# Thresholded attention on one core: the last two groups' queries taken by one-hot products instead of indirect gathers, with a new order of steps

## The chip, the cores and the metric

The kernel runs on one core of one Trainium2 chip. The metric is device time in microseconds (us), lower is better. The engines are named as in the profile: PE (TensorE: matmuls, with PEld for its weight loads), DVE (VectorE), ACT (ScalarE), POOL (GpSimd), SP (SyncE, which here only issues DMA transfers). Each engine takes its instructions in the order in which they were written; the engines wait for each other by semaphores.

## What is computed

```python
batch, heads, seq, dim = 8, 12, 512, 64          # Q, K, V: float32, random normal
scores = np.einsum('bhqd,bhkd->bhqk', Q, K) * (1.0 / np.sqrt(dim))
weights = softmax(scores)                        # exp, max taken off, divided by the row's sum
weights = np.where(weights > threshold, weights, 0)          # threshold = 0.1
weights = weights / (weights.sum(axis=-1, keepdims=True) + 1e-10)
return np.einsum('bhqk,bhkd->bhqd', weights, V)
```

There are 96 heads of 512 queries and 512 keys. A weight of over 0.1 among 512 is rare. Most rows of the output are zero, and a row that is not zero is nearly always one row of V.

## The kernel before, in words

The kernel uses this. It first finds the few query rows ("hits") that can have a weight over the threshold, with cheap arithmetic over all scores; then it does those rows again in float32, finds the key, and copies that row of V to the output. Everything else in the output is filled with zeros by DMA (`do_zero`, SP). A slow general version stands behind a branch at the end and is not taken with these inputs.

Heads are taken in 48 pairs (`hp`), two pairs make a quad (`hq`, 24 of them), and two quads make a group (`j`, 12 of them: 8 heads, 4 pairs). The steps, with the lines that the profile names:

- *Loads* (SP): `load_k` (a pair's K), `load_q` (a quad's Q, tile `q_sb`, one of 4 buffers; partition p holds rows 4p to 4p+3 of each head).
- *Layout*: `ktr` (PE L336) transposes K in float32, `kev` (L319 on ACT, L321 on DVE) copies it to `kt`, `kf` (POOL L323) casts it to half precision; `qmix` (POOL L323 or DVE L321) casts Q, `qtr` (PE L369) transposes it, `qev` copies it to `qt`.
- *Scores*: `qk` (PE L379), `exp` (ACT L385, or a bit trick on DVE, L387) gives `e`; `d` (PE L391, 8 x 4 matmuls per pair) compares every key's exp with the row's sum; `dred` (DVE L399) takes the maximum into `stat`.
- *Once per group, after its fourth `dred`*: `flags` (L403), `size` (PE L412) and `rank` (PE L418, L420) count the hits, `key` (DVE L424) writes each hit's number among its pair's hits (up to 32 slots per pair, 4 pairs: 128 slots), and `oh` (`do_onehot`, DVE L428) compares these numbers with 1 to 32: a one-hot table of 128 partitions by 1024. `idx` (`do_idx`, PE L439, 8 matmuls of the table with a small table of row numbers) gives each slot's row number and which head of the pair it is in; `half` and `idxev` (L448) bring them to SBUF.
- *The hits' queries*: `gather` (POOL, an indirect DMA, L193) fetches the 128 rows of Q from HBM into `qsel`; `split` (L461) puts each into the left or right half of a 128 wide row, by its head; `xtr` (PE L467) transposes that; `xev` copies it to `xq`.
- *Again in float32*: `xqk` (PE L479) scores of the hits, `xexp` (ACT L485) exp and sum, `tv`, `found` (DVE L496) the key over the threshold, `vidx` (L503) its row number, `fetch` (POOL, indirect DMA from V into `vsel`), `scatter` (POOL, indirect DMA from `vsel` into the output).

All indirect DMAs go through one line, the helper's L193, and are told apart by their tiles: `qsel<-in_Q_dram`, `vsel<-in_V_dram`, `out_dram<-vsel`.

The order is written out. Each step is entered by `add` (or `stage`, L619, for a group's steps) with the engines that may do it, an assumed duration, the steps it needs and the buffers that it takes and gives back. `ORDER` (L132) holds two strings found by a search outside of the kernel: the sequence of all 1498 steps, two characters each, and for each step that has a choice the engine. `Schedule.order` turns them into calls. Two PSUM buffers (`sm`) are shared by `d`, `qtr`, `rank`, `idx`, `xtr` and `xqk`; three (`sc`) by `ktr` and `qk`.

`near` (L616) marks the last two groups, 10 and 11, whose hits are only known when hardly any other work is left. 18 `spare` matmuls on a zero tile (L259) may be put between the steps after the last `d`. At the very end of POOL's sequence stand fetch 10, fetch 11, scatter 9, scatter 10 and scatter 11.

Of the kernel before, what the change touches and what calls it, by code (L numbers as in the profile page):

```python
# [55 lines left out]
def kernel(  # L56
# [59 lines left out]
    def by_pairs(ap):  # L116
# [20 lines left out]
        "6d2l4C48473N4o3O3P5q3Q3R4A2k3S3T4D493U3V4N4s4q4O4U4B4E4F4G4H4I4r581q1r4J4K4L4P4V3X3W1s3Y1y4S4v5s4M6b5r5v4T1t1u3Z"
        "5x5D4Q4w5E5u3a5z4g4R5+5Q4t4u5w5y3b3c4W3d4X4Y5B4Z4z3e4x3f5C5-4+3g8X6c7m4a4b604y6H1v4c3h4d3i4e5F594-50615152536454"
        "5A5G5566625H5I5J5K4f6Z1w6563675L565M5N5O6f9g3j6K6L6g575P6i6h6k68696A6B6C6D6M6I6j5S6E6m6l5R6F5T5U6G6N6J3k5V5W5X3l"
        "6O721x3m5Y6P796n7A5Z6o7l7k8W8VAR233n7p5a7r3o6r6t6p6s5b7K5c6u7t6Q6R6q7o7q7s73771z5d7v7u7L74786S6v6w6T6U6V6x756y6W"  # L140
        "6X6z6+6-7w808T6Y769f4k7x707B710w7C7y7D7E818B8a8c3p5e7F7+7G7H7I7z8e8C7J8Z7-8f8G8b5f8283848D858d6a5g3q8U9e7nAPAQ8H"
        "86875h1+889j7M8g9l898I5i8A8J8E8l7N8F7O9n8y5t7P8j8m8k9o8h8z8i8K7Q8L5j7R9i8-8+7S9k7T8n8MBZBa0ICL909m8N7U938O8P8Q8R"
        "9EAT8oBY7V7W8SAN9F9p9194AV9w8p928q8rAX8s8t8u8v9u8w95967XAU9798999v9A9x9BA5AW9CAC9s8x9q9DAYADAa9G9H9I9tAZ9JA8A69r"
        "5k9KA99y9z9+9L9M7YAsA79-AxAfA05mAg7ZB9AA7aBd5lA1Ay7bA2ABA37cAbAc7gAhAv9NA4AEAiAFAGAH9OAIAdAwBcAtAeBeCJCKDU3zBf9P"
        "9QAuBhAJAzAKBgALCNCPA+Bi9RAOCO7dAMBjCRBmBkBlDTCQB-A-B0B1B2B3B4B5BqAjAkB6AlAmBoAnFOBnAoBrApBpB7CHAqCSArC0C6C2BsC1"
        "BtCTDSEDEFC3CUBA9SCmDXBuDZC7BvBwBxBy9TBz9UB+CVCXCY9VCWCZDWB8D2CpDY9WBBBCCaDaBDC4BECqBFCnCbCIBGDbC5C8CcBHDcEBD33r"
        "9a1-CoDdC9CACBCCEI3sDv9XEKCtDgCdG9FMEECDCECeCfCFCgChDeCuDhCGDfDiBICiCjCkCrBJEHDjBKCsClDkEJEMCvCwELENCxCyCzC+9YC-"
        "D0DlD1BLE0DwEOD4ETDmEgDnE1D5DoD6DxFREUDpD77eD8EREnEjDqESEoEkFNHI6e7fFTBMDrDsD9DtDADuEVEPBND+FVBOEWEzEQDBFWBPD-Dy"
        "FQEhEiFSBQEXEYEZEaG7EbDCDzElGBEcG5DDBRECDEEdFU7h5n3tEeEfG8BSGCGDFXGEFcEm2qGFEpEqGGFYFaHHHGI3FdFpFZErEsGHEtE2E3Eu"
        "FeE4EvEw5o7iFbFfE5E6FqE7E8ExE9FgDFGIBUFrI1JCDVI2FsFwFtFhFiFjFkFlFmEyEAFxGaBTE+FnE-GJHLFuHNFoF0FvF1HPF2GNHKGKHQDG"  # L150
        "GbHMDHGOGtF3DIGPHOGcF4GsF5DJGQFyGfGLFzF+DKF-G0G1G2BV5pHRHjF6GhJAJBJzCMGgG6GMGdHUF7F8GiI6G3GRGSHVG4GTGUGVGeGWHkGX"
# [612 lines left out]
```

## Time and profile before

| | |
|---|---|
| median of 3 runs | 208.61 us (207.15 to 209.53) |
| the profiled execution | 208.51 us, of which the span from the first to the last instruction is 206.8 us |
| mean granted TensorE clock | 0.969 |
| DMA | 38.86 MB, mean 188 GB/s |
| chain that ended last | PE 65%, DVE 13%, issue 6%, ACT 5%, DMA 4%, POOL 3% |
| last `dred` (DVE L399) ends | 185.07 us |
| last scatter ends on POOL | 202.55 us |

How to read the profile's lines. In the page, `PE 183.9 (89%) x3235` is busy time, its share of the span and the number of instructions. A group line reads: line, engine, operation, tiles written and read, shapes, number; then busy time and mean nanoseconds of one; then the idle time of the engine just before them with what ended it. A line of the timeline has the start in us from the span's start, the time from the start of the first to the end of the last of the instructions put together in it, then engine, line, operation, tiles, shape, number, and in brackets the engine's idle time before it and what released it; "issue" is a wait for nothing that the profile shows. A line of the table by stretches has the stretch, its length, busy time and number of instructions of PE, PEld, DVE, ACT and POOL, then the granted clock of TensorE (1.00 is full), the DMA's share and GB/s.

### The profile page before, as it was taken

How to read it: one execution, taken by the hardware profiler on the slowest of the kernel's cores; microseconds unless marked ns; L12 is line 12 of the kernel's file. 1: busy time of each engine (PE TensorE's matmuls, PEld its weight loads, DVE VectorE, ACT ScalarE, POOL GpSimd, SP SyncE). 2: the span in 40 equal slices, each digit the busy share in tenths (PEclk: the TensorE clock that was granted, in tenths of full speed). 3: DMA queues.
4: the chain of work that ended last, by engine and by line, in shares of the span. 5: the costliest groups of instructions: out<-in, count | busy, mean ns of one | idle time of the engine just before them, and what ended most of it. 6: DMA issues, size and time to landing. Idle time of an engine off the chain costs nothing.

```text
span 206.8 us, 7766 instructions
## 1 busy us (share of the span) xinstructions
PE 183.9 (89%) x3235; PEld 122.4 (59%) x3237; DVE 171.0 (83%) x320; ACT 163.1 (79%) x194; POOL 108.8 (53%) x176
## 2 busy tenths in 40 slices
PE   7888999999999999999999988899989999868900
PEld 4554758666756677576677566576657567652200
DVE  6679998999889899989999795989979989642650
ACT  2798998979989999998999988879978899601200
POOL 5025046607467419254656776286665666344661
PEclk9999999999999999999999999999999999696995
DMA  6999799783996599749776279999399500000000
GB/s 138 238 288 258 185 257 269 212 224 89 277 338 190 182 284 275 206 109 251 231 236 149 75 204 241 384 394 210 101 323 412 220 6 8 10 8 4 7 13 11
DMA packets 69589, 38.86 MB, mean 188 GB/s; under 512 B 54356, under 2 KB 66276, under 8 KB 69552
## 3 DMA queue, kind: packets, MB, share of 16 engines
q1 hardware_dynamic: 67344, 37.50, 64.4%
q0 software_dynamic: 1152, 0.59, 1.7%
q8 instruction: 26, 0.43, 0.9%
q10 hardware_dynamic: 1056, 0.26, 0.6%
q14 instruction: 11, 0.09, 0.2%
HBM read 25.95 MB, written 12.98 MB: 188 GB/s over the span
## 4 chain that ended last, share of the span: by engine, by line
PE 65%; DVE 13%; issue 6%; ACT 5%; DMA 4%; POOL 3%; another core or an unknown queue 1%; POOLq 1%; SPq 0%; DVEq 0%; ACTq 0%
PE sc L379 22%; PE sm L391 19%; DVE e L387 6%; PE sc L336 5%; PE sm L479 4%; PE sm L412 4%; PE sm L369 3%; ACT e L385 3%; PE sm L439 3%; DMA k_sb<-in_K_dram 2%; DVE stat L399 2%; DVE qt L321 2%; DMA vsel<-in_V_dram,vidx 1%; PE sc L259 1%; POOL out_dram L193 1%
## 5 line engine op out<-in xcount | busy, mean ns | idle before, releaser
L385 ACT ACTIVATE e<-sc 128x1024 bf16<-128x1024 f32 x140 | 135.8, 1031 | 13.0 <-PE sc L379 11.8
L379 PE MATMUL sc<-qt,kf 64*128 64x512 f16 x384 | 65.2, 384 | 4.5 <-DVE e L387 2.8
L391 PEld LDWEIGHTS <-e 128*128 128x128 bf16 x1536 | 52.5, 99 | 24.4 <-issue 23.8
L387 DVE TENSOR_SCALAR e<-sc 128x1024 int16<-128x1024 f32 x52 | 63.2, 1218 | 4.5 <-PE sc L379 3.2
L391 PE MATMUL sm<-groups,e 128*128 128x64 bf16 x1536 | 62.8, 194 | 2.0 <-issue 1.2
L323 POOL CAST kf<-kt 128x512 f16<-128x512 f32 x46 | 29.7, 660 | 45.1 <-ACT kt L319 34.2
L399 DVE TENSOR_REDUCE stat<-sm 128x8 f32<-128x512 f32 x48 | 32.6, 684 | 9.6 <-PE sm L391 3.0
L379 PEld LDWEIGHTS <-kf 64*128 64x128 f16 x384 | 18.9, 94 | 19.5 <-issue 11.2
L323 POOL CAST qm<-q_sb 128x512 f16<-128x512 f32 x40 | 26.9, 684 | 3.2 <-DMA q_sb<-in_Q_dram 3.1
L193 POOL DMA_INDIRECT qsel<-in_Q_dram,idx x12 | 13.3, 1108 | 18.7 <-DVE idx L448 13.7
L336 PE MATMUL sc<-identity_f,k_sb 64*128 64x64 f32 x368 | 19.3, 226 | 0.7 <-DMA k_sb<-in_K_dram 0.7
L336 PEld LDWEIGHTS sc<-identity_f,k_sb 64*128 64x128 f32 x368 | 16.7, 138 | 3.7 <-DMA k_sb<-in_K_dram 1.0
L319 ACT COPY kt<-sc 128x1024 f32<-128x1024 f32 x16 | 16.2, 1013 | 1.4 <-PE sc L379 0.7
L193 POOL DMA_INDIRECT vsel<-in_V_dram,vidx x12 | 12.9, 1076 | 3.3 <-issue 1.6
L321 DVE COPY qt<-sm 128x1024 f16<-128x1024 f16 x20 | 13.6, 682 | 1.2 <-PE sc L379 1.2
L369 PE MATMUL sm<-identity_h,qm 128*128 128x128 f16 x184 | 14.1, 219 | 0.5 <-DVE stat L399 0.5
L193 POOL DMA_INDIRECT out_dram<-vsel,idx x12 | 12.8, 1064 | 3.2 <-issue 2.9
L479 PE MATMUL sm<-kt,xq 128*32 128x512 f32 x96 | 13.7, 642 | 0.9 <-DVE xq L321 0.6
L359 DVE TENSOR_SCALAR qsq<-qt 128x1024 int16<-128x1024 int16 x24 | 13.3, 560 | 0.0
L369 PEld LDWEIGHTS <-qm 128*128 128x128 f16 x184 | 10.6, 97 | 2.6 <-issue 2.2
L412 PE MATMUL sm<-heads,qsq 128*128 128x2 bf16 x192 | 11.0, 163 | 1.0 <-issue 1.0
L412 PE MATMUL sm<-heads,ksq 128*128 128x2 bf16 x192 | 11.4, 165 | 0.5 <-issue 0.5
(94 smaller groups left out, 168.5 us busy)
## 6 DMA issues: line engine op xcount, KB each, us to landing
out_dram<-zero SPq DMA_DIRECT2D x24, 512.0 KB
k_sb<-in_K_dram SPq DMA_DIRECT2D x95, 128.0 KB
q_sb<-in_Q_dram SPq DMA_DIRECT2D x23, 512.0 KB
k_sb<-in_Q_dram SPq DMA_DIRECT2D x3, 128.0 KB
qsel<-in_Q_dram,idx POOLq DMA_INDIRECT x12, 4.5
vsel<-in_V_dram,vidx POOLq DMA_INDIRECT x12, 3.0
out_dram<-vsel,idx POOLq DMA_INDIRECT x12, 2.2
k_sb<-in_K_dram ACTq DMA_DIRECT2D x1, 128.0 KB
```

The lines of the kernel that those rows point to most:

```text
L193: return keep(nc.gpsimd.indirect_dma_start(**args))
L321: keep(nc.vector.tensor_copy(dst, src))
L323: keep(nc.gpsimd.tensor_copy(dst, src))
L336: keep(nc.tensor.matmul(buffer("sc", ("ktr", hq))[:, at:at + D], lhsT=k_sb[rows, r, :, :].rearrange("p h d -> p (h d)"), rhs=identity_f32[ ...
L369: keep(nc.tensor.matmul(buffer("sm", ("qtr", hq))[:].bitcast(f16)[:, at], lhsT=buffer("qm", hq)[:, at], rhs=identity_h[:], is_transpose=Tr ...
L379: keep(nc.tensor.matmul(buffer("sc", ("qk", hp, c))[:, h * S:(h + 1) * S], lhsT=pair("kf", hq)[ps, n, c * P:(c + 1) * P], rhs=pair("qt", h ...
L385: keep(nc.scalar.activation(e[:], sc[:], ACTF.Exp, scale=scale))
L387: keep(nc.vector.tensor_scalar(e[:].bitcast(i16), sc[:], BITS_A, BITS_B, op0=ALU.mult, op1=ALU.add))
L391: keep(nc.tensor.matmul(buffer("sm", ("d", hp))[:, j * G:(j + 1) * G], lhsT=buffer("e", (hp, c))[:, j * P:(j + 1) * P], rhs=groups[:], sta ...
L399: keep(nc.vector.tensor_reduce(T["stat", j][:, n, :], buffer("sm", ("d", hp))[:].rearrange("p (c g) -> p c g", g=G), axis=AX.X, op=ALU.max))
L412: keep(nc.tensor.matmul(rk[:, at:at + 2], lhsT=sq[:, n % 2, r * P:(r + 1) * P], rhs=heads[:], start=True, stop=True))
L479: keep(nc.tensor.matmul(buffer("sm", ("xs", j))[sl, :], lhsT=xq[:, sl], rhs=pair("kt", 2 * j + n // 2)[:, n % 2], start=True, stop=True, t ...
```

## The change

For groups 10 and 11 the gather, the split and the transposition are gone. A new step `sel` (PE) multiplies the query tiles, which are still in SBUF in float32, with the one-hot table: for each pair, each of the four rows of a partition and each head, a product of the head's 128 x 64 query rows with 128 x 32 of the table, added up over the four rows; 32 matmuls per group. For that the table is made in float32 and in another layout (`oh_f`), and `idx` takes float32 row numbers (`row_f`). `idx`, `half` and `idxev` remain, for the scatter and for `vidx`. All other groups are as they were, but the search for an order was continued, so that both strings of `ORDER` are new throughout (1494 steps), with other choices of engine too.

```diff
-        "0401020005060D0BN7N0080t0703N2N5N3090L0J0P0A0M0C0K0u0Q0E0NN4N10F0v200G0H0cN60x210s0O0y0z0d0-0g0a0+0R0S0T120U0V1K"
+        "0204000106050D0B0tN0070803MzM-N1090P0J0L0u0Q0CN20E0v0K0F0A0M0G0N0x0c0O0r0d0y0+200s0z210H0-0a0R0S0T0U0e0V0W0XM+12"
...
+    row_f = consts.tile([P, C2, 5], f32)
...
+        keep(nc.vector.tensor_copy(row_f[:], row_no[:]))
...
     def do_onehot(j, eng):
+        key = keys[:, j, 0:KEY].rearrange("p (n c) -> p n c", n=4)
+        if j >= NO - 2:
+            oh = work.tile([P, C2, 4, SLOTS], f32, name="oh_f")
+            keep(nc.vector.tensor_tensor(
+                out=oh[:], in0=slot_no[:, :, 0].unsqueeze(1).unsqueeze(1).to_broadcast([P, C2, 4, SLOTS]),
+                in1=key.rearrange("p n c -> p c n").unsqueeze(3).to_broadcast([P, C2, 4, SLOTS]), op=ALU.is_equal))
+        else:
...
     def do_idx(j, eng):
+        oh = T["oh", j][:]
...
+            if j >= NO - 2:
+                one, rows = oh.rearrange("p c n s -> p c (n s)")[:, c, :], row_f
+            else:
+                one, rows = oh.rearrange("p n s c -> p c (n s)")[:, c, :], row_no
+            keep(nc.tensor.matmul(ix[:, 0:5], lhsT=one, rhs=rows[:, c, :], start=(c == 0), stop=(c == C2 - 1)))
+
+    def do_sel(j, eng):
+
+        oh = T["oh", j]
+        for n in range(4):
+            q_sb = T["q", 2 * j + n // 2]
+            for r in range(R):
+                for h in range(2):
+                    keep(nc.tensor.matmul(buffer("sm", ("xp", j))[h * D:(h + 1) * D, n * SLOTS:(n + 1) * SLOTS],
+                                          lhsT=q_sb[:, 2 * (n % 2) + h, r, :], rhs=oh[:, h * R + r, n, :],
+                                          start=(r == 0), stop=(r == R - 1), tile_position=(0, h * D)))
...
-        stage("gather", {"POOL": (1.45, 4.2 if near else 6.4, 0.1)}, [("idxev", j)] + ([("split", j - NS)] if j >= NS else []), do_gather)
-        stage("split", {"POOL": (0.4, 0.55), "DVE": (0.21, 0.37)}, [("gather", j), ("half", j)], do_split, takes=[("qb", j)])
-        stage("xtr", {"PE": (0.17, 0.40)}, [("split", j)], do_xtr, takes=[("sm", ("xp", j))], gives=[("qb", j)])
-        stage("xev", {"DVE": (0.2, 0.35), "ACT": (0.2, 0.36)}, [("xtr", j)], do_xev, gives=[("sm", ("xp", j))], takes=[("xq", j)])
+        if near:
+            stage("sel", {"PE": (0.95, 1.2)}, [("oh", j)] + [("q", hq) for hq in (2 * j, 2 * j + 1)], do_sel, takes=[("sm", ("xp", j))], gives=[("oh", j)])
+        else:
+            stage("gather", {"POOL": (1.45, 6.4, 0.1)}, [("idxev", j)] + ([("split", j - NS)] if j >= NS else []), do_gather)
+            stage("split", {"POOL": (0.4, 0.55), "DVE": (0.21, 0.37)}, [("gather", j), ("half", j)], do_split, takes=[("qb", j)])
+            stage("xtr", {"PE": (0.17, 0.40)}, [("split", j)], do_xtr, takes=[("sm", ("xp", j))], gives=[("qb", j)])
+        stage("xev", {"DVE": (0.2, 0.35), "ACT": (0.2, 0.36)}, [("sel" if near else "xtr", j)], do_xev, gives=[("sm", ("xp", j))], takes=[("xq", j)])
...
-        stage("vzero", {"POOL": (0.12, 0.25)}, [("gather", j)], do_vzero, takes=[("vsel", j)])
+        stage("vzero", {"POOL": (0.12, 0.25)}, [("idxev" if near else "gather", j)], do_vzero, takes=[("vsel", j)])
```

In the new order the steps from the last `dred` on stand as follows. PE: `size` 11, `xtr` 9, `rank` 11, `xqk` 9, `idx` 11, `xqk` 10, `sel` 11, `xqk` 11, then spare matmuls. DVE: `flags` 11, `xev` 9, `key` 11, `oh` 11, `idxev` 11, `tv` and `found` 9, `tv` 10, `xev` 11, `found` and `vidx` 10, `tv`, `found` and `vidx` 11. POOL, from gather 9 on: gather 9, scatter 3, scatter 7, `split` 9, scatter 6, scatter 5, scatter 8, `vidx` 9, fetch 9, fetch 10, fetch 11, scatter 9, scatter 10, scatter 11. `sel` 10 stands before the last `d` steps: PE `sel` 10, one `qk`, `idx` 10, `d` 46, `d` 47. Before the change PE had, after the last `d`: `size` 11, `rank` 11, 4 spares, `idx` 11, `xtr` 9, `xtr` 10, `xqk` 9, spares, `xqk` 10, `xtr` 11, `xqk` 11.

More of the change, by code (lines that the diff above doesn't have):

```diff
@@ L137 @@
[L137 to L151, printed above, removed]
@@ L164 @@
+        "0100001000101000000010010011000010001000010000011101000001000010000000010000000101000000000110100000101000100100"
+        "1001011000011000000101010000000100100001000001001101000001000011001000011000000001000001000101000000100001000010"
+        "001000000110001011101011",
     )
```

58 lines of the change are left out of this document (33 added, 25 removed).

## The prediction

> **What bounds the kernel now.** I read the page first, then the table by stretches, then the tail in order of time.
>
> ```profile
> span 206.8 us, 7766 instructions
> PE 183.9 (89%) x3235; PEld 122.4 (59%) x3237; DVE 171.0 (83%) x320; ACT 163.1 (79%) x194; POOL 108.8 (53%) x176
> ```
>
> ```profile
> core 0: us, PE busy (x) PEld busy (x) DVE busy (x) ACT busy (x) POOL busy (x), PEclk, DMA share, GB/s
> 20.00:182.39 162.39, 155.56 (x2952) 108.31 (x2949) 147.15 (x243) 146.71 (x172) 90.53 (x144) 0.99 0.73 209
> 182.39:185.07 2.68, 1.22 (x33) 0.92 (x29) 0.69 (x1) 0.00 (x0) 1.65 (x4) 1.00 0.07 15
> 185.07:206.80 21.73, 10.49 (x61) 3.20 (x62) 8.16 (x28) 2.33 (x7) 9.84 (x12) 0.78 0.05 8
> ```
>
> From 20 us to the last `d` matmul (182.39) three engines are full: PE busy 155.56 of 162.39 us, DVE 147.15, ACT 146.71. I call this the bulk; added work there costs time. From the end of the last `dred` (185.07, called T below) to the end, 21.7 us, no engine is busy for half of the time: that is a chain of single steps for groups 9, 10 and 11.
>
> ```profile
> 179.98 2.41 PE L391 MATMUL sm<-groups,e 128*128 128x64 bf16 x64
> 184.38 0.69 DVE L399 TENSOR_REDUCE stat<-sm 128x8 f32<-128x512 f32 x1 [2.15 <-remote]
> 186.02 0.69 DVE L428 TENSOR_TENSOR oh<-slot_no,keys 128x1024 f16<-128x1024 bf16 x1
> 186.76 0.57 PEld L439 LDWEIGHTS <-oh 128*128 128x128 f16 x8 [0.69 <-DVE oh L428]
> 188.21 1.08 POOL L193 DMA_INDIRECT qsel<-in_Q_dram,idx  x1 [3.82 <-DVE qb L461]
> 188.59 1.94 PE L479 MATMUL sm<-kt,xq 128*32 128x512 f32 x8
> 192.18 0.29 DVE L461 TENSOR_TENSOR qb<-qsel,half 128x128 f32<-128x128 f32 x1
> 193.30 0.29 DVE L321 COPY xq<-sm 128x128 f32<-128x128 f32 x1
> 193.74 1.07 PE L479 MATMUL sm<-kt,xq 128*32 128x512 f32 x8 [0.26 <-DVE xq L321]
> 194.91 0.60 ACT L485 ACTIVATE xe<-sm 128x512 f32<-128x512 f32 x1 [1.75 <-issue]
> 195.41 0.19 ACT L485 ACTIVATION_READ_ACCUMULATOR xe<-sm 128x1 f32 x1
> 195.87 1.04 POOL L193 DMA_INDIRECT vsel<-in_V_dram,vidx  x1 [0.30 <-issue]
> 197.62 1.01 POOL L193 DMA_INDIRECT vsel<-in_V_dram,vidx  x1 [0.71 <-issue]
> 201.57 0.98 POOL L193 DMA_INDIRECT out_dram<-vsel,idx  x1 [0.30 <-issue]
> ```
>
> Group 11's one-hot ends at 186.71; its queries are split only at 192.18. These 5.5 us hold `idx`, `half`, the gather (issued 188.21) and its landing. The last fetch is issued at 197.62, T+12.55. Behind it stand three scatters, and the span ends 9.2 us later; that part stays, since fetches and scatters of the last three groups keep their order at the end of POOL.
>
> **The change part by part.** *Group 11 after T.* Flags, rank and key stay: 0.95 us from T to the one-hot's start. Then come `oh` (now float32), `idx`, `xqk` of group 10 (it stands between them in the new order), `sel`, `xev`, `xqk`, `xexp`.
>
> ```profile
> L461 DVE TENSOR_TENSOR qb<-qsel,half 128x128 f32<-128x128 f32 x4 | 1.1, 283 | 0.0
> L424 DVE TENSOR_TENSOR keys<-sm,flags 128x96 bf16<-128x96 f32 x12 | 3.0, 251 | 1.9 <-PE sm L420 0.9 <-PE sc L379 0.9
> L439 PE MATMUL sm<-row_no,oh 128*128 128x5 f16 x96 | 7.6, 202 | 0.2 <-DVE oh L428 0.2
> L439 PEld LDWEIGHTS <-oh 128*128 128x128 f16 x96 | 7.0, 165 | 2.6 <-DVE oh L428 1.8 <-issue 0.9
> 191.34 1.06 PE L479 MATMUL sm<-kt,xq 128*32 128x512 f32 x8 [0.27 <-ACT xe L485]
> ```
>
> - `oh`: two-tensor operations with float32 grow by 32 ns from 96 to 128 elements (251, 283), 1 ns per element; 1024 elements give 1.2 us. Lower end 0.69, the half-precision form shown above.
> - `idx`: 8 float32 matmuls. L479 shows 8 records for the 4 matmuls of one step, so a float32 matmul is two passes: 16 here. The 8 strided loads of L439 (186.76) took 0.57 us; less the last one's own 0.165, over 7 steps, one load of 128 columns with its 5-column matmul takes 58 ns. 16 of them give 0.95, I take 1.0 (now 0.5).
> - `sel`: 32 float32 matmuls, so 64 passes, each loading 64 columns and streaming 32. A load is 58 x 64/128 = 29 ns. The streaming: 1.06 us less the 0.2 that a short matmul takes alone (L439 202 ns), over two rounds of 512 columns, is 0.84 ns a column, 27 ns for 32. A pass is 56 ns. The four column groups of L479 run at once (one after another, 8 passes of 0.43 would be 3.4 us, not 1.06), and `sel` alternates two column groups, so I halve it: 32 x 56 = 1.8 us, plus 0.2 until it can be read. Upper end 64 x 56 = 3.6.
>
> Chain from T: 0.95 + oh 1.2 = 2.15; idx 0.05 + 1.0 = 3.2; xqk 10 1.06 = 4.26; sel 2.0 = 6.26; xev 0.05 + 0.29 = 6.6; xqk 11 0.1 + 1.06 = 7.76; xexp 0.1 + 0.69 = 8.55; from its end to the fetch as now (195.60 to 197.62) 2.02 = 10.6. Against 12.55 this is 1.95 us earlier, not 5.5: `oh`, `idx`, another group's `xqk` and `sel` fill the gap. The queue of POOL allows it: a fetch holds it for 1.3 us (1.01 and 0.30 before it), fetches 9 and 10 are ready earlier by the two other groups' `xqk`, and scatters 6, 5 and 8 now stand before fetch 9, in time in which POOL has nothing else.
>
> *The clock in that chain.*
>
> ```profile
> 176.81:180.22 3.41, 3.41 (x49) 2.56 (x49) 2.13 (x5) 2.26 (x4) 1.04 (x1) 0.50 0.04 10
> 183.64:187.05 3.41, 1.88 (x23) 1.07 (x25) 1.82 (x4) 0.00 (x0) 0.71 (x3) 1.00 0.02 3
> 187.05:190.46 3.41, 3.30 (x18) 0.80 (x17) 0.93 (x4) 0.27 (x1) 1.95 (x2) 0.50 0.02 3
> ```
>
> After the thin stretch 183.64 to 187.05 the granted clock is 0.50 for 3.41 us, and `xqk` of group 9 takes 1.94 us there instead of 1.06. The new order has no spare matmul ahead of `sel` 11 (now four stand after `rank`), so I let the same stretch be slow. With T at 186.57 (below), `oh` ends at 188.72, xqk 9 at 189.2, and `idx` 11 runs at half speed to 190.8 instead of 189.7: +1.1 us. Ends: 0, and +3 if `xqk` 10 and half of `sel` fall into a slow stretch too. [...]
>
> *The bulk.* Counted in the two programs' orders: PE gets `sel` 10 (1.8) and the longer `idx` 10 (+0.5) ahead of the last `d`, +2.3. ACT gets 3 exps more, 2 `half` more, one `qt`, one `kf`, two `xq` copies fewer. DVE loses 3 exps and gets 5 `qmix`, 5 `vidx`, one `qt`, one `kf`, two `xq` and the longer `oh` 10. POOL loses 2 gathers, 5 `qmix`, 5 `vidx`.
>
> ```profile
> L385 ACT ACTIVATE e<-sc 128x1024 bf16<-128x1024 f32 x140 | 135.8, 1031 | 13.0 <-PE sc L379 11.8 <-DVE tv L491 0.6
> L387 DVE TENSOR_SCALAR e<-sc 128x1024 int16<-128x1024 f32 x52 | 63.2, 1218 | 4.5 <-PE sc L379 3.2 <-PE sc L336 1.1
> L321 DVE CAST qm<-q_sb 128x512 f16<-128x512 f32 x6 | 3.2, 546 | 0.3 <-DMA q_sb<-in_Q_dram 0.3
> L321 DVE COPY qt<-sm 128x1024 f16<-128x1024 f16 x20 | 13.6, 682 | 1.2 <-PE sc L379 1.2
> L503 DVE TENSOR_SCALAR vidx<-kept,half 128x1 int32<-128x1 f32 x2 | 0.4, 214 | 0.1
> L319 ACT COPY qt<-sm 128x1024 f16<-128x1024 f16 x3 | 3.1, 1023 | 0.0
> L323 POOL CAST qm<-q_sb 128x512 f16<-128x512 f32 x40 | 26.9, 684 | 3.2 <-DMA q_sb<-in_Q_dram 3.1
> ```
>
> ACT: 3 x 1.03 less one `qt` 1.02 and about 0.8 of small copies, +1.3. DVE: -3.65 + 5 x 0.546 + 5 x 0.214 + 0.68 (`qt`) + about 1.2 (`kf`, `xq`, `half`, `split`) + 0.5 (`oh` 10) = +2.5. So PE, DVE and ACT all get 1.3 to 2.5 us more, POOL 7 to 8 less (5 x 0.684, 2 x 1.08, the rest small). If their idle shares stay, T moves by the mean, +2; idle time of the three (7, 15 and 16 us of 162.39) could take it all. I take +1.5, nearer to the load, since PE, the fullest, gets `sel` 10 in its last 6 us, where `d` 46 and `d` 47 queue behind it. Ends: 0 and +2.3.
>
> *What costs nothing.*
>
> ```profile
> qsel<-in_Q_dram,idx POOLq DMA_INDIRECT x12, 4.5
> out_dram<-vsel,idx POOLq DMA_INDIRECT x12, 2.2
> ```
>
> These are us from issue to landing. `half` and `idxev` of groups 10 and 11 no longer gate a gather, only scatters. `idxev` 10 waits on DVE until scatter 3 has landed (it frees the index buffer), and scatter 3 now stands right behind gather 9 on POOL: 1.08 + 0.3 + 1.0 + 2.2, some 4.6 us after `idxev` 9. Before `idxev` 10 can run it needs `oh` 10, `sel` 10 and `idx` 10 anyway (1.2 + 2.0 + 1.0) and three shorter steps, so the wait is covered; without that cover one `qsq` and the last two `dred` behind it come up to 0.5 us later. `xtr` 9 now stands on PE ahead of `rank` 11, `xev` 9 on DVE ahead of `key` 11; they need gather 9 (4.5 us), which is issued ahead of `sel` 10, `idx` 10 and two `d` (6 us), and run beside `dred`, `flags` and `rank`. If that gather were late, the whole chain would wait for it. `xev` 10 stands on ACT ahead of the last exp and waits for `sel` 10; PE has 2.2 us of `idx` 10 and `d` 46 meanwhile, more than that exp. SP issues the same loads and zero stores in another sequence; after 182.39 the DMA moves 8 to 15 GB/s, so two gathers fewer free nothing there. The last four query loads have no successor, so holding their tiles blocks no load. One small cast for `row_f` runs beside the first loads.
>
> *Sum.* The profiled execution took 208.51 us, 206.8 of it span; the median of the runs shown is 208.61, so they agree. 208.51 + 1.5 - 1.95 + 1.1 = 209.2 us, its own range 207.5 to 210.6.
>
> **The rivals.** (1) *`sel` runs one pass after another* and ends slower than before: 3.6 us instead of 1.8, twice (once in PE's last stretch, once in the chain), 212.8 us. For it: float32 weights of changing tile positions occur nowhere in this trace but in L479. Against: L479 overlaps. It decides from about 2.6 us per `sel` (+0.8 twice, past 210.7). [...]
>
> (2) *The 2 us at the last `dred` do not come back.* `d` 47 ends at 182.39, but DVE is released only at 184.38, by what the profile calls remote; PE then runs the 2-column matmuls of `size` 11 and stands still twice (one of the two: below). The new order has the same run there, so I keep the loss; without it 207.2 us.
>
> ```profile
> 183.60 0.23 PE L412 MATMUL sm<-heads,ksq 128*128 128x2 bf16 x3 [0.47 <-issue]
> ```
>
> (3) *The bulk does not grow* (POOL's relief pays for it) *and the tail's clock stays full*: 208.51 - 1.95 = 206.6; with (2) too, 204.6.
>
> **How the numbers follow.** About no change, 209.2: 0.43. Rival (1): 0.26, with a `sel` under half a clock (+1.9, 211.1) counted here. Rival (2): 0.14. Rival (3), with or without (2): 0.17. A measurement of this kernel can tell about 1% (206.5 to 210.7 is no change). Slower: (1) plus the forecast's upper edge, 0.31. Faster: (3) plus part of (2), 0.24. The rest, 0.45, within 1%. Range 205.2 to 212.6: it leaves out the ends of (1) and (3), a tenth each.
>
> **What would show it.** `sel` 11: its 64 passes about 28 ns apart (right) or 56 (rival 1). `oh_f` 1.2 us. T (end of the last `dred`) near 186.6; `idx` 11 under a clock of 0.50; last fetch at T+11.7, last scatter 4 us behind it. The forecast is wrong if T stays at 185 or below, or `sel` takes over 2.6 us.

## The result and the profile after

The changed kernel took 214.94 us (median of 4 runs, 213.78 to 218.38) beside 208.55 us of the kernel before on the same chip: ratio 1.029, 95% interval 1.021 to 1.038. It is slower; 209.2 was forecast, 212.6 was the upper end. The profiled execution took 213.78 us (before 208.51). Ratios and intervals, here and below, leave out a kernel's unusually slow executions, while medians count all of them, so the two need not agree exactly.

Page of the changed kernel, its span and the busy time of the engines:

```profile
span 212.1 us, 8055 instructions
PE 194.9 (92%) x3378; PEld 133.7 (63%) x3379; DVE 172.1 (81%) x329; ACT 163.8 (77%) x195; POOL 103.6 (49%) x163
```

The same execution by stretches, cut at the start of group 10's key step (`key` 10), at the end of the last `dred` (T) and at the issue of the last fetch:

```profile
core 0: us, PE busy (x) PEld busy (x) DVE busy (x) ACT busy (x) POOL busy (x), PEclk, DMA share, GB/s
20.00:176.28 156.28, 150.95 (x2863) 105.08 (x2861) 142.36 (x245) 144.28 (x169) 84.12 (x132) 1.00 0.76 219
176.28:188.57 12.29, 10.91 (x176) 9.53 (x176) 6.53 (x10) 3.76 (x5) 6.74 (x9) 0.72 0.04 8
188.57:203.43 14.86, 12.56 (x126) 7.40 (x128) 6.57 (x19) 2.23 (x7) 2.44 (x3) 0.69 0.03 4
203.43:212.10 8.67, 3.66 (x15) 1.27 (x13) 2.28 (x7) 0.00 (x0) 4.00 (x4) 0.89 0.05 11
```

The kernel before, cut in the same way:

```profile
20.00:176.45 156.45, 150.06 (x2837) 103.69 (x2834) 142.64 (x233) 143.58 (x168) 88.37 (x142) 1.00 0.75 217
176.45:185.07 8.62, 6.72 (x140) 5.54 (x140) 5.19 (x11) 3.12 (x4) 3.82 (x6) 0.80 0.05 10
185.07:197.62 12.55, 10.12 (x59) 3.09 (x60) 6.36 (x23) 2.33 (x7) 5.83 (x8) 0.86 0.03 5
197.62:206.80 9.18, 0.38 (x2) 0.11 (x2) 1.80 (x6) 0.00 (x0) 4.01 (x4) 0.67 0.08 13
```

So the span's 5.3 us come as -0.17 up to `key` 10, +3.67 from there to T, +2.31 from T to the last fetch, -0.51 behind it. All of the loss stands behind `key` 10.

What stands there, from the timeline of the changed kernel (start, duration, engine, line, operation; L432 is the float32 one-hot, L459 `sel`, L450 `idx`, L393 `d`, L501 `xqk`):

```profile
176.57 1.97 DVE L432 TENSOR_TENSOR oh_f<-slot_no,keys 128x1024 f32<-128x1024 bf16 x1
178.59 2.06 PE L459 MATMUL sm<-oh_f,q_sb 128*64 128x32 f32 x64 [1.23 <-DVE oh_f L432]
181.12 3.57 PE L450 MATMUL sm<-row_f,oh_f 128*128 128x5 f32 x16
184.55 3.30 PE L393 MATMUL sm<-groups,e 128*128 128x64 bf16 x64
187.88 0.69 DVE L401 TENSOR_REDUCE stat<-sm 128x8 f32<-128x512 f32 x1 [0.67 <-PE sm L393]
189.74 2.01 DVE L432 TENSOR_TENSOR oh_f<-slot_no,keys 128x1024 f32<-128x1024 bf16 x1
191.80 1.95 PE L450 MATMUL sm<-row_f,oh_f 128*128 128x5 f32 x16 [1.33 <-DVE oh_f L432]
193.68 1.47 PE L501 MATMUL sm<-kt,xq 128*32 128x512 f32 x8
195.09 3.63 PE L459 MATMUL sm<-oh_f,q_sb 128*64 128x32 f32 x64
199.20 1.94 PE L501 MATMUL sm<-kt,xq 128*32 128x512 f32 x8 [0.48 <-DVE xq L323]
203.43 1.00 POOL L193 DMA_INDIRECT vsel<-in_V_dram,vidx  x1 [2.18 <-DVE vidx L525]
207.37 0.98 POOL L193 DMA_INDIRECT out_dram<-vsel,idx  x1 [0.30 <-issue]
```

Ahead of T, PE waits 1.23 us for group 10's one-hot, then runs `sel` 10, `idx` 10 and only then the last 64 `d` matmuls, for which the last `dred` waits. Behind T the one-hot takes 2.0 instead of the forecast 1.2, `idx` 11 1.95 instead of 1.0, `sel` 11 3.63 instead of 2.0. The loss of about 2 us ahead of the last `dred` in the kernel before is not here: `d` 47 ends at 187.85, `dred` starts at 187.88.

The clock, in stretches of 3.41 us, at whose edges it changed in this trace (same columns as above):

```profile
177.15:180.56 3.41, 2.19 (x66) 1.95 (x64) 3.28 (x4) 1.80 (x2) 2.94 (x4) 1.00 0.03 8
180.56:183.97 3.41, 3.41 (x20) 2.96 (x16) 0.26 (x1) 1.37 (x3) 2.93 (x6) 0.50 0.05 13
183.97:187.38 3.41, 3.41 (x58) 3.41 (x58) 1.47 (x4) 0.07 (x1) 0.00 (x0) 0.50 0.02 4
187.38:190.80 3.42, 2.79 (x63) 1.72 (x60) 2.48 (x5) 0.26 (x1) 0.00 (x0) 1.00 0.02 5
190.80:194.21 3.41, 2.41 (x24) 2.02 (x24) 1.13 (x2) 0.59 (x3) 0.00 (x0) 1.00 0.00 0
194.21:197.62 3.41, 3.41 (x56) 2.54 (x50) 1.07 (x5) 0.69 (x2) 1.43 (x2) 0.50 0.00 0
```

Two windows in which PE had little to do (busy for 2.19 and 2.41 of 3.41 us) are followed by half clock (0.50), one with 2.79 us is not. The busy time alone does not decide this: in the same trace the window from 122.53, busy for 2.44 us, kept the full clock (more in the last section). Under half clock fall `idx` 10 and the last `d`, and later `sel` 11 and `xqk` 11.

The pair above ran on one chip, the experiments on four others, each run beside the kernel before on its own chip, where that took 199.1 to 199.9 us. Ratios are therefore compared, and the stretches of the kernel before and of the changed one were taken again on one of those chips (fifth and sixth run).

### The profile page after: what moved, and what is told of

It reads as the page before. It is cut to its first block, busy times and chain, and to the rows that moved or that the text cites. A ratio compares the mean times of both kernels' runs of the same rounds, so it can differ in the third digit from the quotient of the medians.

```text
span 212.1 us, 8055 instructions
## 1 busy us (share of the span) xinstructions
PE 194.9 (92%) x3378; PEld 133.7 (63%) x3379; DVE 172.1 (81%) x329; ACT 163.8 (77%) x195; POOL 103.6 (49%) x163
## 4 chain that ended last, share of the span: by engine, by line
PE 58%; issue 13%; POOL 10%; DVE 7%; ACT 7%; DMA 3%; ACTq 0%; POOLq 0%; DVEq 0%
PE sc L381 21%; PE sm L393 18%; ACT e L387 5%; PE sc L338 5%; DVE e L389 5%; PE sm L371 4%; POOL out_dram L193 4%; PE sm L414 3%; PE sm L501 3%; POOL vsel L193 3%; DMA k_sb<-in_Q_dram 2%; PE sm L450 2%; DVE stat L401 2%; ACT kt L321 1%; DMA vsel<-in_V_dram,vidx 1%
## 5 line engine op out<-in xcount | busy, mean ns | idle before, releaser
L387 ACT ACTIVATE e<-sc 128x1024 bf16<-128x1024 f32 x143 | 138.2, 1034 | 14.3 <-PE sc L381 9.9
L393 PEld LDWEIGHTS <-e 128*128 128x128 bf16 x1536 | 53.3, 99 | 20.1 <-issue 19.2
L393 PE MATMUL sm<-groups,e 128*128 128x64 bf16 x1536 | 63.6, 195 | 0.9 <-DVE stat L401 0.8
L389 DVE TENSOR_SCALAR e<-sc 128x1024 int16<-128x1024 f32 x49 | 59.6, 1218 | 5.1 <-PE sc L381 4.5
L325 POOL CAST qm<-q_sb 128x512 f16<-128x512 f32 x35 | 21.8, 640 | 4.1 <-DMA q_sb<-in_Q_dram 4.0
L193 POOL DMA_INDIRECT qsel<-in_Q_dram,idx x10 | 12.2, 1217 | 13.8 <-DVE idx L470 13.7
L507 ACT ACTIVATE xe<-sm 128x512 f32<-128x512 f32 x12 | 7.3, 608 | 13.6 <-PE sm L501 8.2
L323 DVE COPY qt<-sm 128x1024 f16<-128x1024 f16 x21 | 14.4, 684 | 1.0 <-PE sm L371 0.7
L501 PE MATMUL sm<-kt,xq 128*32 128x512 f32 x96 | 14.1, 659 | 1.0 <-DVE xq L323 1.0
L361 DVE TENSOR_SCALAR ksq<-kf 128x1024 int16<-128x1024 int16 x24 | 11.7, 491 | 0.0
L259 PE MATMUL sc<-warm 128*128 128x512 bf16 (+1 forms) x30 | 9.6, 455 | 1.7 <-DVE warm L222 1.2
```

The lines of the kernel that those rows point to most:

```text
L193: return keep(nc.gpsimd.indirect_dma_start(**args))
L323: keep(nc.vector.tensor_copy(dst, src))
L325: keep(nc.gpsimd.tensor_copy(dst, src))
L387: keep(nc.scalar.activation(e[:], sc[:], ACTF.Exp, scale=scale))
L389: keep(nc.vector.tensor_scalar(e[:].bitcast(i16), sc[:], BITS_A, BITS_B, op0=ALU.mult, op1=ALU.add))
L393: keep(nc.tensor.matmul(buffer("sm", ("d", hp))[:, j * G:(j + 1) * G], lhsT=buffer("e", (hp, c))[:, j * P:(j + 1) * P], rhs=groups[:], sta ...
```

## The experiments

My theory was that the time goes to the work put behind the keys: float32 `idx`, the slow one-hot, `sel` 10 ahead of the last `d`, and to the half clock, which I took to come with such thin work. One rival was that the newly searched order is worse by itself, the other that the clock alone costs it.

**One: `idx` from a half-precision table.** Changed kernel; one more one-hot step per group, only `sel` reads the float32 one.

```diff
-        else:
-            oh = work.tile([P, 4, SLOTS, C2], f16)
+            T["oh", j] = oh
+        oh = work.tile([P, 4, SLOTS, C2], f16)
...
+        T["oh16", j] = oh
...
-        oh = T["oh", j][:]
+        oh = T.pop(("oh16", j))[:].rearrange("p n s c -> p c (n s)")
```

> The changed kernel, except that `idx` 10 and 11 load a half-precision one-hot table of their own (one more VectorE step of 0.69 us for each of the two groups) and only `sel` reads the float32 one. Theory (what costs is the work put on TensorE behind the keys, the float32 loads of `idx` first): the 16 passes go from 111 and 213 ns to about 60 or 120, `idx` 10 from 3.57 to 0.5 to 1.0 and `idx` 11 from 1.95 to 0.5 to 0.6 with a start 0.7 later; last `dred` 2.5 us earlier, the end 3 us earlier: about 211.5, 0.985 of the changed kernel. Rival 'the newly searched order is worse by itself': no gain, 214.5 to 215.5. Rival 'it is the granted clock alone': the thinner `idx` leaves TensorE idler, the half-clock windows stay, and the gain is 1 us or less: 214.

Measured: 205.84 us, 1.037 of the kernel before (1.030 to 1.044); the unaltered changed kernel stands at 1.048 (fifth run). `idx` 10 on the timeline of this run:

```profile
177.92 0.66 PE L446 MATMUL sm<-row_no,oh 128*128 128x5 f16 x8
```

0.66 instead of 1.95 at full clock (fifth run): the price of float32 `idx` is shown, 1.29 us per group. The ratio fell by about 1%, though the two intervals still overlap (1.030 to 1.044 and 1.040 to 1.055); most of the loss stayed.

**Two: spare matmuls to hold the clock.** Changed kernel with five spare matmuls of 512 columns ahead of each `idx` and `sel` of groups 10 and 11.

```diff
+    def hot(buf, n):
+        for i in range(n):
+            keep(nc.tensor.matmul(buf[:, 0:S], lhsT=warm[:, 0:P], rhs=warm[:, 0:S], start=True, stop=True))
...
+        if j >= NO - 2:
+            hot(ix, 5)
...
+        hot(buffer("sm", ("xp", j)), 5)
```

> The changed kernel with 5 spare 512-column matmuls, into the product's own PSUM buffer, ahead of each of `idx` 10, `idx` 11, `sel` 10 and `sel` 11; nothing else differs. Rival 'the clock alone': the windows at 0.5 behind 180.56 and 194.21 go, `idx` 10 from 3.57 to 1.95, `d` 46 and 47 from 3.30 to 2.41, `sel` 11 from 3.63 to 2.06, `xqk` 11 from 1.94 to 1.06, 5.0 us together, less some 2.1 for the spare matmuls that do not fall into a wait (those ahead of `idx` 10 and `sel` 11): 212, 0.985 of the changed kernel. Theory 'the work itself': about half of that at most, since 1.95 for `idx` and 2.0 for the float32 one-hot stay at full clock: 213 to 214.5, above the kernel before in either case. If thin matmuls do not hold the clock even behind spare ones, the windows stay and it is 216.

Measured: 209.31 us, 1.054 of the kernel before (1.048 to 1.060): no gain. In the profiled execution (207.08 us) the clock stayed full (table by stretches):

```profile
185.00:190.00 5.00, 4.80 (x36) 2.65 (x36) 2.01 (x6) 1.03 (x5) 0.30 (x1) 1.00 0.00 0
190.00:195.00 5.00, 4.51 (x80) 2.77 (x81) 1.83 (x6) 0.69 (x2) 2.13 (x2) 1.00 0.04 8
```

`sel` 11 took 2.06 again, but each set of spare matmuls held PE for 1.25 us, and those ahead of `idx` 10 and `sel` 11 stood in the chain, 2.5 us together. The clock alone does not explain the loss: with a full clock the kernel took 207.08 us, 4.0% more than the kernel before (199.13), and without those 2.5 us, by estimate, it would still be 2.7% more.

**Three: adjacent slot numbers.** Changed kernel; the float32 one-hot compares with 32 adjacent numbers instead of every eighth element.

```diff
+    slot_f = consts.tile([P, SLOTS], bf16)
...
-                out=oh[:], in0=slot_no[:, :, 0].unsqueeze(1).unsqueeze(1).to_broadcast([P, C2, 4, SLOTS]),
+                out=oh[:], in0=slot_f[:].unsqueeze(1).unsqueeze(1).to_broadcast([P, C2, 4, SLOTS]),
```

> The changed kernel, except that the float32 one-hot compares with a slot table of 32 adjacent elements instead of every eighth element (16 bytes apart) of the old one. If the stride is what makes the step 2.0 us instead of the 1.2 predicted, it falls to about 1.2, twice, and the end comes 0.8 to 1.6 earlier: 213.3 to 214. If it is the 1024 float32 results or the three-fold broadcast pattern, it stays at 2.0 and the time at 214.9.

Measured: 207.62 us, 1.045 (1.040 to 1.050), which can't be told from the changed kernel's 1.048. The step itself, by its tile (minimum, median, maximum in ns):

```profile
L434 DVE TENSOR_TENSOR oh_f<-slot_f,keys x2: 1224/1224/1225, 173.1 to 184.1; 128x1024 f32<-128x1024 bf16 x2
```

1.224 us, where nothing but the layout of the slot numbers was changed: the stride of 16 bytes made it 2.0. The gain in time was not seen; in this run's profile `idx` 10 and `d` 46 and 47 (3.35 us) ran partly at half clock.

**Four: the old order.** Kernel before with the changed kernel's one-hot, `idx` and `sel`; gathers and splits of groups 10 and 11 fall away, `sel` stands where `xtr` stood.

```diff
-        stage("gather", {"POOL": (1.45, 4.2 if near else 6.4, 0.1)}, [("idxev", j)] + ([("split", j - NS)] if j >= NS else []), do_gather)
+        stage("gather", {"POOL": (1.45, 4.2 if near else 6.4, 0.1)}, [("idxev", j)] + ([("split", j - NS)] if j >= NS else []), skip if near else do_gather)
...
-        stage("xtr", {"PE": (0.17, 0.40)}, [("split", j)], do_xtr, takes=[("sm", ("xp", j))], gives=[("qb", j)])
+        stage("xtr", {"PE": (0.17, 0.40)}, [("split", j)], do_sel if near else do_xtr, takes=[("sm", ("xp", j))], gives=[("qb", j)])
```

> The order of the kernel before, not searched again: gathers and splits of groups 10 and 11 left out, the float32 one-hot and the float32 `idx` as in the changed kernel, and `sel` 10 and 11 at the places where `xtr` 10 and 11 stood, the first behind `idx` 11 and `xtr` 9, with the spare matmuls of the old order still between them. Theory 'the work itself': last `dred` 1.5 to 3 late by the one-hot (+1.3) and `idx` 10 (+1.4 to 3); from it to the last fetch about 16 (2.35 + 1.3 + 1.4 to the end of `idx` 11, then 2.06 + 1.06 + 1.06 + 2.0 + 1.06 and spare matmuls of 1.4, then 2.3): 212 to 216, no better than the changed kernel. Rival 'the newly searched order is the cost': near the kernel before, 208 to 210.

Measured: 212.92 us (median of 4 runs: 209.19, and 212.63 to 213.31) beside 199.13, without an interval. Even the shortest execution is 5% above the kernel before, as far as the changed kernel (1.048), so the rival "the order alone" falls. The three longer ones, at 7%, are worse than I expected of my own theory: in the profiled one (213.22) `idx` 11 (3.57), `sel` 10 (3.63) and an `xqk` (1.94) stood in a row under half clock between T and `sel` 11.

**Five and six: the two kernels again on one chip.** No edit.

> The changed kernel again, unaltered, beside the kernel before on one chip, as a standard for the four runs above, which were on another chip than the first pair. With float32 `idx` and the strided table removed one at a time the ratios were 1.037 and 1.045; if both cost what they showed, the changed kernel stands at 1.045 to 1.055 here. If it stands at 1.03 as in the first pair, those two edits gained nothing in sum and the theory that the work behind the keys costs the time is in doubt.

> The kernel before, unaltered, with a profile on the same chip: from the last exponential to last `dred`, and from there to the last fetch. If the first pair's 2 us lost ahead of last `dred` belong to that execution alone, they are missing here, and the kernel before ends about 2 us earlier against the changed one than the first pair showed.

Measured: changed kernel 208.42 us, 1.048 of the kernel before (1.040 to 1.055); kernel before 199.05 us. The kernel before, then the changed one, cut as above:

```profile
20.00:169.30 149.30, 147.78 (x2835) 103.27 (x2833) 142.58 (x233) 142.56 (x168) 87.47 (x142) 1.00 0.78 227
169.30:175.93 6.63, 6.63 (x144) 5.32 (x144) 5.33 (x11) 3.81 (x5) 3.28 (x4) 0.74 0.05 11
175.93:187.99 12.06, 8.97 (x64) 2.96 (x60) 6.88 (x23) 2.33 (x7) 7.05 (x12) 1.00 0.04 7
187.99:197.30 9.31, 0.38 (x2) 0.11 (x2) 1.80 (x6) 0.00 (x0) 4.02 (x4) 0.63 0.07 13
```

```profile
20.00:171.96 151.96, 148.49 (x2831) 103.26 (x2829) 144.38 (x244) 143.22 (x168) 83.59 (x131) 1.00 0.77 225
171.96:181.18 9.22, 8.53 (x204) 7.40 (x200) 6.82 (x10) 4.45 (x6) 6.65 (x9) 1.00 0.04 11
181.18:196.10 14.92, 12.97 (x127) 7.40 (x128) 6.56 (x19) 2.23 (x7) 2.44 (x4) 0.69 0.03 4
196.10:204.70 8.60, 3.58 (x15) 1.27 (x13) 2.26 (x7) 0.00 (x0) 4.01 (x4) 0.90 0.06 11
```

Here the 7.4 us of the span come as +2.66 up to `key` 10, +2.59 to T, +2.86 to the last fetch, -0.71 behind it. Up to `key` 10 there is no product of the change yet: the first 2.66 belong to the new order, with its other choices of engine. DVE is busy 1.8 us more and PE stands idle 1.95 us more in that stretch (3.47 of 151.96 us against 1.52 of 149.30). The 2 us ahead of the last `dred` are missing in the kernel before here. The clocks differ, so two of the differences need care. Ahead of T it is the kernel before that had half clock (0.74), and the tenth and twelfth runs show the same steps at full clock in 5.76 us. Behind T it is the changed kernel (0.69): `xqk` 10, `sel` 11 and `xqk` 11 took 1.54, 3.63 and 1.94 us in place of 1.06, 2.06 and 1.06, together 2.9 more, as much as the whole +2.86. At full clock, by this estimate, the chain behind T would have neither gained nor lost; the dearer one-hot and `idx` (some 0.8 and 0.9 more than forecast) took up most of the forecast gain.

**Seven: three prices lowered.** Changed kernel and order, with the edits of runs one and three together (for group 11 the half-precision table first) and 3 and 4 spare matmuls in the waits ahead of `sel` 10 and `idx` 11.

```diff
+        if j == NO - 1:
+            hot(ix, 4)
...
+        if j == NO - 2:
+            hot(buffer("sm", ("xp", j)), 3)
```

> The changed kernel and its order, with three prices of the change lowered at once: `idx` 10 and 11 from a half-precision table of their own (made first for group 11), the float32 table from 32 adjacent slot numbers (1.22 instead of 2.0), and 3 and 4 spare matmuls in the waits ahead of `sel` 10 and `idx` 11. Theory 'the work behind the keys': against the changed kernel `idx` 10 -2.6, the clock under `d` 46 and 47 -0.9, the table -0.8 for group 11, `idx` 11 -0.8 (it starts 0.7 later but hides under the table), the clock under `sel` 11 and `xqk` 11 -2.5: some 6 to 7 us less than the changed kernel, which is about the time of the kernel before, 0.995 to 1.015 of it. Rival 'the new order or the bulk itself': 2 to 3% stay.

Measured: 202.19 us, 1.016 of the kernel before (1.010 to 1.022).

```profile
20.00:171.80 151.80, 148.35 (x2831) 103.26 (x2829) 144.18 (x245) 143.06 (x168) 83.42 (x131) 1.00 0.76 225
171.80:179.80 8.00, 7.92 (x199) 6.33 (x194) 6.54 (x11) 4.44 (x6) 6.35 (x9) 1.00 0.05 12
179.80:189.93 10.13, 9.50 (x128) 5.11 (x129) 6.38 (x19) 2.22 (x7) 2.44 (x4) 1.00 0.04 6
```

From T to the last fetch it is 10.13, 1.93 us less than in the kernel before: the gain of 1.95 that the prediction worked out is there once the one-hot and `idx` are cheap and the clock is full. That it comes so close is partly chance: both chains are 0.5 us shorter here than in the prediction (10.13 for 10.6, 12.06 for 12.55). What stays is +2.5 up to `key` 10 and +1.37 to T. So the theory gets most of it, and the rival of the order has a part after all.

**Eight: group 11 alone.** Order of the kernel before; group 10 gathers. `sel` 11 is moved ahead of `xqk` 10, its eviction to ACT. The order is kept as coded text, so its changes are given here and below as PE's steps.

```diff
-        stage("xtr", {"PE": (0.17, 0.40)}, [("split", j)], do_xtr, takes=[("sm", ("xp", j))], gives=[("qb", j)])
+        stage("xtr", {"PE": (0.17, 0.40)}, [("oh" if last else "split", j)], do_sel if last else do_xtr, takes=[("sm", ("xp", j))], gives=[] if last else [("qb", j)])
...
-PE: xqk 9, spare x2, xqk 10, spare x3, xtr 11, spare, xqk 11
+PE: xqk 9, sel 11, xqk 10, xqk 11
```

> The order of the kernel before with one-hot products for group 11 alone: group 10 is gathered as before, so nothing is put ahead of last `dred`. Group 11: half-precision table, `idx` 11, float32 table from adjacent slots, then `sel` 11 right behind `xqk` 9, ahead of `xqk` 10; its eviction moves to ScalarE and the scatter of group 8 ahead of the fetches. If the removal of the last gather is worth what the prediction says once `sel` 10 and the float32 `idx` are out of the way, `xqk` 11 ends 7.5 to 8.5 us behind last `dred` instead of 9.7, and the time is 1 to 2 us below the kernel before (0.99 to 0.995). If thin `sel` matmuls bring the half clock (3.6 instead of 2.06, `xqk` 1.94 instead of 1.06), the gain is gone: 1.000 to 1.005.

Measured: 202.46 us, 1.015 (1.006 to 1.024): a miss. On the timeline:

```profile
181.28 2.06 PE L464 MATMUL sm<-oh_f,q_sb 128*64 128x32 f32 x64 [0.81 <-ACT xe L512]
187.14 1.02 POOL L193 DMA_INDIRECT vsel<-in_V_dram,vidx  x1 [2.77 <-DVE tv L518]
188.47 1.01 POOL L193 DMA_INDIRECT vsel<-in_V_dram,vidx  x1 [0.30 <-issue]
```

`sel` 11 needs a PSUM buffer that group 9's exponentials hold (wait of 0.81), and `xqk` 10 behind it makes fetch 10 late; fetch 11 stands right behind fetch 10 on POOL. The gather was replaced by a wait for another group, so nothing was gained: this profiled execution took 199.31 us, the kernel before 199.25. The other three took 201.14 to 205.08; two of them had a mean clock of 0.95 to 0.96 against 0.98, and no profile shows where they lost it.

**Nine: both groups, old order up to `idx` 10.** The mended prices, the order of the kernel before for the bulk, the changed kernel's order for the tail.

```diff
-PE: idx 10, qk, qk, d 46, d 47, size 11, rank 11, spare x4, idx 11, spare, xtr 9, xtr 10, xqk 9, spare x2, xqk 10, spare x3, xtr 11, spare, xqk 11
+PE: idx 10, qk, qk, sel 10, d 46, d 47, size 11, xtr 9, rank 11, xqk 9, spare x4, idx 11, xqk 10, sel 11, xqk 11
```

> One-hot products for groups 10 and 11 at the mended prices (half-precision `idx`, adjacent slots), with the order of the kernel before up to `idx` 10 and the changed kernel's order behind it: `sel` 10 ahead of `d` 46, `xtr` 9 and `xqk` 9 around `rank` 11, then `idx` 11, `xqk` 10, `sel` 11, `xqk` 11, four spare matmuls ahead of `idx` 11. Theory 'the newly searched order lengthens the stretch up to `key` 10 by 2.5 us, the products themselves do not': `key` 10 at 169.3 as in the kernel before, then 8.0, 10.1 and 9.2 us as in the mended run: span 196.6, 0.993 to 1.000 of the kernel before. Rival 'the products cost it in whatever order': 1.012 to 1.02 like the mended run.

Measured: 199.60 us, 1.000 of the kernel before (0.996 to 1.003), against 1.016 with the new order.

```profile
20.00:169.86 149.86, 147.83 (x2835) 102.97 (x2833) 142.39 (x234) 142.54 (x168) 86.73 (x143) 1.00 0.78 227
169.86:178.12 8.26, 7.26 (x200) 6.21 (x199) 6.34 (x12) 4.08 (x6) 5.55 (x7) 1.00 0.06 11
178.12:188.75 10.63, 9.68 (x129) 5.31 (x131) 7.00 (x21) 2.06 (x6) 2.89 (x6) 1.00 0.04 7
```

`key` 10 is back at 169.86. With the products in place and the old order it is where the kernel before has it, so the new order, not the products, costs the 2.5 us ahead of `key` 10. Runs one to four, all on one chip, point the same way: 171.82 to 173.27 in the new order, 170.34 in the old. Against the kernel before in the sixth run, what is won behind T (12.06 to 10.63) is lost ahead of it (6.63 at a clock of 0.74, or 5.76 at full clock, to 8.26, with `sel` 10 on PE).

**Ten and twelve: group 11 alone, tail put in another order.** Only group 11 by products, so that nothing stands ahead of T; `xtr` 9 and `xqk` 9 behind `rank` 11, `sel` 11 behind `xtr` 10. The twelfth run has seven spare matmuls in waits in place of two.

```diff
-PE: size 11, rank 11, spare x4, idx 11, spare, xtr 9, xtr 10, xqk 9, spare x2, xqk 10, spare x3, xtr 11, spare, xqk 11
+PE: size 11, spare x2, rank 11, xtr 9, xqk 9, idx 11, xtr 10, sel 11, xqk 10, xqk 11
+PE (twelfth run): size 11, spare x3, rank 11, xtr 9, spare x2, xqk 9, idx 11, spare x2, xtr 10, sel 11, xqk 10, xqk 11
```

> One-hot products for group 11 alone, again in the order of the kernel before up to last `dred`, but with the tail put in another order than in the run before: `xtr` 9 and `xqk` 9 behind `rank` 11, `idx` 11, `xtr` 10, `sel` 11, `xqk` 10, `xqk` 11; evictions of 9, 10, 11 on ScalarE, split 10 on GpSimd, two spare matmuls ahead of `rank` 11 and none behind. No wait for another group's exponentials stands ahead of `sel` 11 now. `key` 10 at 169.2, last `dred` 175 to 176, last fetch some 10.1 behind it (0.95 + 0.69 + 1.22 + 2.06 + 0.5 + 1.06 twice + 0.8 + 2.0 with hand-overs), span 194.5 to 195.5: 0.984 to 0.992 of the kernel before. If the clock goes to half under `sel` 11 and both `xqk` (+1.6 and +1.8): 0.998 to 1.006.

> The run before with group 11 alone, with seven spare matmuls in place of two: three ahead of `rank` 11, two behind `xtr` 9 (while its eviction is awaited), two behind `idx` 11 (while the float32 table is finished). Nothing else moves. If the half clock under `sel` 11, `xqk` 10 and `xqk` 11 (3.63 and 3.43 us for the last two together) came from the thin stretch between last `dred` and `idx` 11, they fall to 2.06 and 1.9, the last fetch comes 10 to 10.5 behind last `dred`, and all executions are like the shortest of the run before (197.5): 0.987 to 0.993 of the kernel before. If `sel` itself lets the clock fall, spare matmuls ahead of it change nothing and it stays at 0.998 to 1.003, with 0.5 in the clock column behind last `dred`.

Measured: tenth run 200.35 us, 0.998 (0.993 to 1.003), its executions from 197.52 to 201.26; twelfth run 197.67 us, 0.989 (0.9845 to 0.9935), from 197.01 to 197.87. The profiled execution of the tenth run is one of its longer ones (200.85). Tenth run first, then the twelfth: `sel` 11, the two `xqk`, the last fetch, and the clock windows (the one ahead of `sel` 11 first):

```profile
179.84 3.63 PE L464 MATMUL sm<-oh_f,q_sb 128*64 128x32 f32 x64
183.40 3.43 PE L506 MATMUL sm<-kt,xq 128*32 128x512 f32 x16
189.83 1.01 POOL L193 DMA_INDIRECT vsel<-in_V_dram,vidx  x1 [0.31 <-issue]
176.24:179.66 3.42, 2.45 (x26) 1.25 (x25) 2.61 (x5) 1.04 (x4) 3.02 (x6) 1.00 0.03 7
179.66:183.07 3.41, 3.41 (x62) 3.23 (x62) 0.95 (x4) 0.27 (x1) 2.62 (x5) 0.50 0.03 9
```

```profile
179.92 2.06 PE L464 MATMUL sm<-oh_f,q_sb 128*64 128x32 f32 x64
181.91 1.92 PE L506 MATMUL sm<-kt,xq 128*32 128x512 f32 x16
187.11 1.01 POOL L193 DMA_INDIRECT vsel<-in_V_dram,vidx  x1 [0.30 <-issue]
176.29:179.71 3.42, 3.26 (x31) 1.39 (x29) 2.61 (x5) 1.03 (x4) 3.03 (x6) 1.00 0.03 7
```

`sel` 11 starts at nearly the same time, and it and the two `xqk` take 1.57 and 1.51 us less with five more spare matmuls in waits: the half clock came with the thin stretch ahead of `sel` (PE busy for 2.45 us against 3.26), not with `sel` itself. The other executions agree: 2 of the tenth kernel's 12 were below 198 us, all 6 of the twelfth's, though on another chip. The ratio came out as expected, the last fetch did not: it stands 11.36 us behind T, not 10 to 10.5, right behind fetch 10 on POOL.

The twelfth kernel takes about 1% less than the kernel before, and the interval is clear of 1. How much of that is the product's is not shown. In the profiled executions of the twelfth and the sixth run the stretch from T to the last fetch is 0.70 us shorter (11.36 for 12.06, both at full clock), and 0.87 us are won ahead of T (5.76 for 6.63), where nothing of the change stands and the sixth run had half clock. No run keeps group 11's gather with the new tail and the new places of the spare matmuls.

**Eleven: run seven without its spare matmuls.** `hot(...)` taken out again, nothing else.

> The mended kernel (half-precision `idx`, adjacent slots, order of the changed kernel) without its seven spare matmuls. If these only filled waits and the clock does not need them: as the mended one, 1.012 to 1.02 of the kernel before. If a thin stretch ahead of `idx` 11 costs the clock one window, `sel` 11 and an `xqk` run at half speed for part of it, as in the run with half-precision `idx` alone (0.8 and 0.8 us): 1.02 to 1.03, with 0.5 in the clock column somewhere behind last `dred`.

Measured: 201.34 us, 1.012 (1.006 to 1.018), not to be told from run seven; the clock column shows 1.00 from `key` 10 to the last fetch. With the shorter wait for the one-hot and the short `idx`, no window there lost the clock in this execution, so a need for the spare matmuls is not shown.

## Why the prediction was wrong, step by step

In the first pair the span grew by 5.3 us, where +0.65 was forecast (1.5 - 1.95 + 1.1). Of the 4.6 us between, 2.0 came up to T (+3.50 instead of +1.5), 3.2 between T and the last fetch (+2.31 instead of -0.85), and 0.5 were won behind it. So two steps failed: the load ahead of T taken as a mean over a long stretch, and the prices and the clock in the chain behind T.

- *The bulk, +1.5 at T (ends 0 and +2.3): failed.* T came 3.50 us later in the first pair and 5.25 later in runs five and six. I averaged what PE, ACT and DVE get more, as if most of it lay in a stretch with idle time to take it up. Up to `key` 10 the change was -0.17 in the first pair and +2.66 in runs five and six (run nine shows the latter as the order's), just past the upper end. Behind `key` 10 the mean does not hold: there one-hot 10, `sel` 10, `idx` 10 and `d` 46 and 47 are a chain on which every microsecond counts, and it added 2.59 (3.67 in the first pair, under half clock). By the mean I had counted only a third of `sel` 10 and `idx` 10 there, and no wait for the one-hot.
- *`idx` at 58 ns a pass: wrong.* 16 float32 passes took 1.95 us, 111 ns apart at full clock. I had the 58 ns from half-precision loads and carried them over to float32. The loads of `idx` 11, 128 columns each, start 60 ns apart in half precision (kernel before, from 186.76) and 111 in float32 (changed kernel, from 191.80); the 8 half-precision passes of `idx` 10 took 0.66 us in the first run, for 1.95 in float32. It was +0.95 twice at full clock.
- *One-hot 1.2 us: the slope was right, the operand was not.* 1.224 with adjacent slot numbers, 2.0 with a stride of 16 bytes, +0.8 twice.
- *`sel` 2.0 us: right at full clock, by luck.* It took 2.06 us, two passes every 58 ns, so 29 ns a pass (28 forecast). But the forecast had a pass as 29 ns of load, from the half-precision row that failed for `idx`, and 27 ns of streaming. By the float32 rows of `idx` a load of 64 columns alone would be some 55 ns (half of 111, an estimate), 3.5 us for 64 one after another, more than the 2.06 measured; so the two column groups do overlap, as assumed: the two passes of a pair start 6 to 7 ns apart. A pair came every 58 ns at full clock (`sel` 10) and every 107 ns at half clock (`sel` 11), where `idx` loads came every 213; whether loads or streaming set that pace is not shown. The forecast's proof of the overlap from `xqk` went round in a circle, since its 0.43 us a pass already took the groups as running at once. Rival (1), passes one after another, did not happen. The half clock under `sel`, which I had counted with it (+1.9), did: `sel` 11 took 3.63 us in the first pair, more than the 2.6 named as a sign of being wrong.
- *The clock, +1.1 on `idx` 11: right kind, wrong place and size.* `idx` 11 ran at full clock. Instead `xqk` 10, `sel` 11 and `xqk` 11 lost 0.4, 1.6 and 0.9, and ahead of T `idx` 10 and the last `d` lost 1.6 and 1.3 (1.95 and 2.03 at full clock in the fifth run). I looked for thin stretches behind T only. Ahead of T PE waited 1.23 us for one-hot 10 in a window that was then followed by half clock; in the fifth run the wait was 0.62 us, and the same program kept the full clock there.
- *The chain behind T, 10.6 without the clock: its steps were right, several prices were not.* Measured 14.86: +0.2 to the key (an eviction of group 9 stands ahead of it on DVE), +0.8 one-hot, +0.9 `idx`, +0.4 `xqk` 10, +1.6 `sel`, +0.9 `xqk` 11, -0.5 to the fetch, which no longer queues behind another. With a cheap one-hot and `idx` and a full clock it was 10.13 (run seven).
- *Rival (2): its event happened* (the 2 us ahead of the last `dred` vanished), *but was swallowed*. Rival (3) did not happen.

Two things stay open: by what steps the new order takes 2.5 us more up to `key` 10, and why on the first chip both kernels reached `key` 10 at the same time, 4.3 and 7.2 us later than in runs five and six (176.28 and 176.45 against 171.96 and 169.30).

## What to carry to other kernels

A removed transfer is worth the chain that it leaves, not its own latency: price each substitute step from a row with the same type and the same operand layout, since half-precision and float32 loads of 128 columns differed by almost a factor of two here (60 and 111 ns from start to start). Work moved ahead of the last steps of the bulk counted in full here (9.22 us from `key` 10 to T in the fifth run, 5.76 in the tenth and twelfth, all at full clock), however idle the engines were on average; choose how much to move by that (one group, with the tail's order and the spare matmuls changed too, gained 1%, two groups nothing). Read the clock window by window, and try spare matmuls in waits alone: with seven of them there `sel` 11 took 2.06 us (twelfth run), with two 3.63 (tenth run); in the chain, two sets of five cost 2.5 us (second run). Measure whether they are needed: the eleventh run kept the full clock from `key` 10 to the last fetch without those seven of the seventh run.
